# A hybrid diffusion step in fp32 on one core: the RG-LRU layer's units and engines reordered

## The chip, the cores and the metric

The kernel runs on one core of a Trainium2 chip. The metric is the device time of one execution in microseconds. The core's engines work through separate queues, each in order: TensorE (PE in the profile), VectorE (DVE), ScalarE (ACT), GpSimd (POOL), and SyncE (SP), which here only issues DMAs. They wait for one another through semaphores.

## The reference, cut to what matters

The reference is one inference step of a backbone of two layers over 128 context tokens and 512 latent tokens of width 1024. Layer 0 has an SSD mixer and a differential attention, layer 1 a bidirectional RG-LRU mixer; a gated ConvFFN follows each. The change concerns layer 1's mixer alone:

```python
def rglru_direction(xr, wa, ba, wx, bx, lam, h0, reverse):
    r = sigmoid(blockdiag(xr, wa) + ba)
    i = sigmoid(blockdiag(xr, wx) + bx)
    log_a = -RG_C * r * softplus(-lam)
    a = exp(log_a)
    u = sqrt(-expm1(2.0 * log_a)) * (i * xr)
    # linear scan h[n] = a[n] * h[n-1] + u[n], from h0, forward or backward
...
def odd_mixer(h, w_in, conv_w, conv_b, ...):
    gate, xr = split(h @ w_in, 2)
    xr = dwconv_centred(xr, conv_w, conv_b)
    yf = rglru_direction(xr, ..., False)
    yb = rglru_direction(xr, ..., True)
    return ((yf + yb) * gelu(gate)) @ w_out
```

The gate weights wa and wx are 16 blocks of 64x64 for each direction.

## The kernel before, in words

Activations lie transposed: 128 channels by NT = 644 columns (128 context tokens, a gap of 4 columns, 512 latent tokens). An fp32 product is made of three matmuls of a high and a low half (`mm3`, lines 469 to 473), each over two halves of 322 columns (`HALVES`). H is the list of eight pairs (`hhi[t]`, `hlo[t]`) of the mixer's input, and later of its output.

In `odd` (lines 1690 to 1882) 16 units make `h @ w_in`: x0 to x7 for the recurrence and g0 to g7 for the gate. The first three come from `gemm_parts` (line 642), the next twelve from `gemm` (line 484), the last from `last_gate` (line 1838). Their order is `lru_order` (line 426), and their weights are queued in the same order in `items`. A weight block of 128x1024 is loaded by SP (line 103), and `block` (line 122) splits it: ACT casts the high half (line 112) and POOL subtracts the low half in four pieces (line 117). Three blocks are split at a time, so the end of a unit releases the split of the unit three places on.

The program order is written out by a clock. `tick` (line 442) counts 2 for each of the 8 slices of K of a unit, so 16 for a unit, and fires what `after(n, f)` has queued for that tick (line 438); of two steps due at one tick, the one queued first goes first. The engines then take their instructions in that order, whatever the real time is.

Each x unit ends in `recur(t, ps)` (line 1730), which makes xr with one ACTIVATE and three VectorE steps (`conv_into`, line 519) and queues, for each direction d, at ticks from the table `LRU` (line 52; `LRU_LAST`, line 51, for t = 7):
- `product(d, i)` (line 1735): two matmuls of the gate weights `bd` with xr into the two small PSUM tiles, which ACT empties with tanh. The second gate (i = 1) is due 2 ticks behind the first. Behind the last product of a t, `gates_in(t + 3)` issues four DMAs for the gate weights of t + 3 on SP.
- `decay(d)` (line 1748): exp and tanh on ACT.
- `forms(d)` (line 1755): four steps on VectorE, the first of them inv * 0.5 + 0.5.
- `factors(d)` (line 1762): e = 2 inv - 1 on ACT, and a multiplication on POOL.

For both directions together follow `roots` (line 1767: square roots on ACT, which change its table, and multiplications on POOL), the scans (line 1775, VectorE; their sum on POOL) and `gated` (line 1788, VectorE). In the prediction (t, d, i) names a product and (t, d) the other steps. A g unit ends in `gelu(t, ps)` (line 1808): a square on ACT, a VectorE step, 5 ticks on a tanh on ACT, 7 ticks on a VectorE step.

From the last unit on, `give_h` (line 1831) hands the results over as H[t], one half of the columns at a time, with a cast on ACT and a subtraction on VectorE. Then `out_parts` (line 662) multiplies them with `w_out`: for its first three columns slices 0 to 5, then H[6], then H[7], which `ready` (line 1857) splits last.

Of the kernel before, what the change touches and what calls it, by code (L numbers as in the profile page):

```python
# [9 lines left out]
F32 = mybir.dt.float32  # L10
F32R = mybir.dt.float32r
AF = mybir.ActivationFunctionType
OP = mybir.AluOpType
# [34 lines left out]
FAST = (2, 2, 2, 2, 2, 1)  # L48
FFN = (4, 3, 4, 3, 4, 4)
LRU_RATES = 26  # L50
LRU_LAST = (10, 18, 4, 7, 12, 33, 41, 46)
LRU = (14, 31, 4, 7, 14, 51, 59, 66)
GIVE = (1, 4)
TAIL = (8, 5)
ATT = (6, 8, 4, 3, 3, 2, 3, 5, 7, 4)
# [7 lines left out]
def pieces(eng, op, out, a, b, n=PIECE):  # L63

    w = out.shape[-1]
    m = -(-w // n)
    for i in range(m):
        c = slice(w * i // m, w * (i + 1) // m)
        getattr(eng, op)(out[:, c], a[:, c], b[:, c])
# [13 lines left out]
class Weights:  # L83
# [38 lines left out]
    def block(self, i):  # L122
        raw = self.raw.pop(i)
        if self.items[i][3] == "held":
            hi, lo = (self.over.tile(list(raw.shape), F32R, name=f"{p}{i}") for p in ("hi", "lo"))
            self.nc.scalar.copy(hi, raw)
            for k0 in range(0, raw.shape[1], 2):
                q = slice(k0, min(raw.shape[1], k0 + 2))
                self.nc.gpsimd.tensor_sub(lo[:, q], raw[:, q], hi[:, q].bitcast(F32))
            self.parts[i] = hi, lo  # L130
        else:
            self.parts[i] = self.split(self.pool, raw, "w", self.n_part, self.nc.gpsimd)
        self.freed += 1

    def add_up(self, i):
# [105 lines left out]
def tile_hybrid_step(ctx: ExitStack, tc: tile.TileContext, a, o):  # L241
    nc = tc.nc
    k = Core()
# [72 lines left out]
    def fma(out, in0, scalar, in1, op0=OP.mult, op1=OP.add, **kw):  # L316
        nc.vector.scalar_tensor_tensor(out, in0, scalar, in1, op0=op0, op1=op1, **kw)  # L317
# [45 lines left out]
    def add_w(ap, r0, kt, c0, w=128, kind=None):  # L363
        items.append((ap[r0:r0 + 128 * kt, c0:c0 + w], kt, w, kind))
# [58 lines left out]

    ffn_starts = ffn_items(0)
    lw_in, lw_out = a["lru_w_in"][0], a["lru_w_out"][0]
    lru_order = [(what, t) for t in range(7) for what in "xg"]
    lru_order[13:] = [("x", 7), ("g", 6), ("g", 7)]
    for what, t in lru_order:
        add_w(lw_in, 0, 8, 128 * t + (1024 if what == "x" else 0))
    for n in range(8):  # L430
        add_w(lw_out, 0, 8, 128 * n, kind=held(n, N_STD[2]))
    ffn_items(1)
# [5 lines left out]
    def after(n, f):  # L438
        heapq.heappush(k.events, (k.clock + n, k.count, f))
        k.count += 1  # L440
# [73 lines left out]
    def conv(pool, ps, cw, cb, ntaps, t, nt, tag, bufs):  # L514
        out = pool.tile([128, NT], F32, name=tag, tag=tag, bufs=bufs)
        conv_into(out, ps, cw, cb, ntaps, t, nt)
        return out
# [32 lines left out]
    def mtile(tag=None):  # L550
        if tag is None:
            tag = k.m_tags.pop(0)
            k.m_tags.append(tag)
        return k.psum.tile([128, 512], F32, name="mt", tag=tag, bufs=1)
# [1135 lines left out]
    def odd():  # L1690
        with ExitStack() as st:
# [3 lines left out]
            pool = k.tmp = lctx.enter_context(tc.tile_pool(name="lru", bufs=1))  # L1695
# [3 lines left out]
            for b in bd:  # L1699
                nc.gpsimd.memset(b, 0.0)  # L1700
            cols = pool.tile([128, 6, 2, 8], F32, name="lcols")
            minus = pool.tile([128, 1], F32, name="minus")
            cb = [cols[:, i].rearrange("p d t -> p (d t)") for i in range(6)]
            hba, hbx, s2, s4 = range(4)

# [9 lines left out]
            def col(i, d, t):  # L1715
                return cols[:, i, d, t:t + 1]

            def gates_in(t):
                b = bd[t % 3]
                for i, nm in enumerate(("lru_wa", "lru_wx")):  # L1720
                    for s in range(2):
                        r = slice(64 * s, 64 * s + 64)
                        nc.sync.dma_start(b[r, :, i, r], a[nm][0, :, 2 * t + s].rearrange("d k j -> k d j"))

            def tmp(tag, bufs=1):
                return pool.tile([128, NT], F32, name=tag, tag=tag, bufs=bufs)

            gys, opened, k.scanned = {}, {}, set()

            def recur(t, ps):  # L1730

                xr = conv(pool, ps, "lru_cw", "lru_cb", 4, t, 8, "xr", 3)
                hs = []

                def product(d, i):
                    if i == 0:
                        hs.append([])
                    w = tmp("t%d" % i, 6)
                    hs[d].append(w)
                    for c0, c1 in HALVES:  # L1740
                        ps = mtile()
                        nc.tensor.matmul(ps[:, :c1 - c0], bd[t % 3][:, d, i], xr[:, c0:c1], start=True, stop=True)
                        nc.scalar.activation(w[:, c0:c1], ps[:, :c1 - c0], AF.Tanh, scale=0.5,
                                             bias=col(hba if i == 0 else hbx, d, t))
                    if d and i and t < 5:
                        gates_in(t + 3)

                def decay(d):
                    t1 = hs[d][0]
                    inv, e = tmp("inv", 3), tmp("e", 6)  # L1750
                    nc.scalar.activation(inv, t1, AF.Exp, scale=col(s4, d, t), bias=col(s4, d, t))
                    nc.scalar.activation(t1, t1, AF.Tanh, scale=col(s2, d, t), bias=col(s2, d, t))
                    hs[d] += [inv, e]

                def forms(d):
                    t1, t2, inv, e = hs[d]
                    nc.vector.tensor_scalar(inv, inv, 0.5, 0.5, op0=OP.mult, op1=OP.add)
                    fma(e, t1, 1.0, inv, op0=OP.subtract, op1=OP.mult)
                    fma(inv, e, 2.0, inv, op0=OP.add, op1=OP.mult)
                    fma(t2, t2, 1.0, xr, op0=OP.add, op1=OP.mult)  # L1760

                def factors(d):
                    t1, t2, inv, e = hs[d]
                    nc.scalar.activation(e, inv, AF.Identity, scale=2.0, bias=minus)
                    pieces(nc.gpsimd, "tensor_mul", t2, t2, inv)

                def roots():
                    for t1, t2, inv, e in hs:
                        nc.scalar.activation(t1, t1, AF.Sqrt, scale=-1.0)
                    for t1, t2, inv, e in hs:  # L1770
                        pieces(nc.gpsimd, "tensor_mul", t2, t2, t1)
                        nc.gpsimd.memset(e[:, NP:S0], 0.0)
                        nc.gpsimd.memset(t2[:, NP:S0], 0.0)

                def scan(d):
                    t1, t2, inv, e = hs[d]
                    if d == 0:
                        nc.vector.tensor_copy(t2[:, S0 - 1:S0], par("h0", t))
                        nc.vector.tensor_tensor_scan(t1, e, t2, 0.0, op0=OP.mult, op1=OP.add)
                        nc.vector.tensor_copy(last[:, 0, t:t + 1], t1[:, NP - 1:NP])  # L1780
                        return
                    nc.vector.tensor_tensor_scan(t1[:, ::-1], e[:, ::-1], t2[:, ::-1], par("h1", t),
                                                 op0=OP.mult, op1=OP.add)
                    nc.vector.tensor_copy(last[:, 1, t:t + 1], t1[:, 0:1])
                    y = gys[t] = tmp("gy", 8)
                    pieces(nc.gpsimd, "tensor_add", y, hs[0][0], t1)

                def gated():
                    if t not in opened:
                        after(1, gated)  # L1790
                        return
                    fma(gys[t], gys[t], 0.5, opened.pop(t), op0=OP.mult, op1=OP.mult)
                    k.scanned.add(t)

                pace = LRU_LAST if t == 7 else LRU
                for d in range(2):
                    at = pace[d]
                    after(at, lambda d=d: product(d, 0))
                    after(at + 2, lambda d=d: product(d, 1))
                    after(at + pace[2], lambda d=d: decay(d))  # L1800
                    after(at + pace[3], lambda d=d: forms(d))
                    after(at + pace[4], lambda d=d: factors(d))
                after(pace[5], roots)
                after(pace[6], lambda: scan(0))
                after(pace[6] + 1, lambda: scan(1))
                after(pace[7], gated)
# [11 lines left out]
                after(7, end)  # L1818

            for t in range(3):  # L1820
                gates_in(t)
            nc.gpsimd.memset(minus, -1.0)

            def sink(what, t):
                return lambda ps: (recur if what == "x" else gelu)(t, ps)
# [3 lines left out]
                sink(*u)(gemm(H)[0])  # L1829

            def give_h(t, c0, c1):
                if t not in k.scanned:
                    after(1, lambda: give_h(t, c0, c1))
                    return
                split_into(H[t], gys[t][:, c0:c1], c0, c1)
                k.n_given += 1
# [145 lines left out]
```

## Time and profile before

| | us |
|---|---|
| median of 3 runs | 2086.69 |
| lowest and highest run | 2076.94, 2088.32 |
| the profiled execution | 2080.74 |
| its span, first to last instruction | 2078.7 |
| RG-LRU layer, from the convolution of x1 to H[7] | 1336.0 to 1527.1 of the span |

In the profile's rows L471 is a line of the kernel. A row of the timeline gives start, duration, engine, line, operation, output<-input, and in brackets how long the engine had been idle and what released it. A row of the waits gives who waited for whom, how long in all, how often and the longest. A row of the groups gives busy time and the mean of one in ns, and behind a bar the idle time ahead of them.

### The profile page before, as it was taken

The page shows a single profiled execution, that of the slowest core. Times are in us where ns is not written, and L with a number is a line of the kernel's source. Part 1 is how long each engine was busy: PE and PEld are TensorE (multiplying, and loading weights), DVE is VectorE, ACT ScalarE, POOL GpSimd, SP SyncE. Part 2 cuts the span into 40 slices and gives each one's busy share as a digit, 9 for nine tenths or more (in the row PEclk, how much of TensorE's full clock was granted, in tenths as well). Part 3 has the DMA queues.
Part 4 walks back from the last instruction along what each step waited for, and adds up shares of the span by engine and source line. Part 5 has one row for each costly group of instructions (what it writes and reads, how often), then busy time and mean ns, then how long its engine had stood idle before and what let it go on. Part 6 is the DMA issues. An engine that isn't in the chain of part 4 may idle for free. (4 is left out here: it accounts for less than half of the span.)

```text
span 2078.7 us, 33613 instructions
## 1 busy us (share of the span) xinstructions
PE 1880.9 (90%) x12601; PEld 1719.6 (83%) x12601; DVE 1415.1 (68%) x2438; ACT 964.7 (46%) x1677; POOL 1184.0 (57%) x1528
## 2 busy tenths in 40 slices
PE   6878889999998999899999998988779899999997
PEld 4767668888887888798899997977679799999996
DVE  3477765655665337777778786676857778787874
ACT  3454453445444325433334344677725443443445
POOL 3235454333335445576557876478865577776772
PEclk9889999999999999999999999999889899999999
DMA  9554432112113342345542223112121122322221
GB/s 261 174 166 156 147 109 78 44 50 56 49 48 107 111 152 82 102 131 181 174 136 73 82 85 97 39 49 56 31 61 48 44 71 81 88 78 72 61 82 71
DMA packets 255577, 196.59 MB, mean 95 GB/s; under 512 B 13837, under 2 KB 233816, under 8 KB 255288
## 3 DMA queue, kind: packets, MB, share of 16 engines
q1 hardware_dynamic: 252664, 184.59, 29.6%
q0 software_dynamic: 2528, 7.13, 1.4%
q8 instruction: 99, 1.62, 0.3%
q10 hardware_dynamic: 224, 2.73, 0.3%
q14 instruction: 62, 0.51, 0.1%
HBM read 187.50 MB, written 6.92 MB: 94 GB/s over the span
## 5 line engine op out<-in xcount | busy, mean ns | idle before, releaser
L117 POOL TENSOR_TENSOR wlo<-wraw,whi 128x256 fp32r<-128x256 f32 (+1 forms) x835 | 710.7, 880 | 562.2 <-ACT whi L112 497.9
L471 PE MATMUL wide<-hhi,whi 128*128 128x322 f32 (+4 forms) x1072 | 358.7, 335 | 34.1 <-DVE X L317 15.2
L472 PE MATMUL wide<-hlo,whi 128*128 128x322 f32 (+4 forms) x1072 | 344.0, 321 | 7.5 <-DVE hlo L512 7.3
L473 PE MATMUL wide<-hhi,wlo 128*128 128x322 f32 (+4 forms) x1072 | 341.6, 319 | 0.0
L112 ACT CAST whi<-wraw 128x1024 fp32r<-128x1024 f32 (+1 forms) x259 | 217.4, 840 | 146.2 <-PE wide L473 71.1
L471 PEld LDWEIGHTS wide<-hhi,whi 128*128 128x128 f32 x1072 | 211.3, 197 | 52.9 <-ACT shi L112 15.4
L471 PE MATMUL gh<-hhi,whi 128*128 128x322 f32 (+3 forms) x688 | 232.1, 337 | 8.7 <-ACT zt L1178 8.7
L472 PEld LDWEIGHTS wide<-hlo,whi 128*128 128x128 f32 x1072 | 211.3, 197 | 12.2 <-DVE hlo L512 8.2
L472 PE MATMUL gh<-hlo,whi 128*128 128x322 f32 (+3 forms) x688 | 216.4, 315 | 1.3 <-DVE hlo L512 1.0
L473 PE MATMUL gh<-hhi,wlo 128*128 128x322 f32 (+3 forms) x688 | 215.9, 314 | 0.0
L473 PEld LDWEIGHTS wide<-hhi,wlo 128*128 128x128 f32 x1072 | 211.1, 197 | 0.0
L317 DVE SCALAR_TENSOR_TENSOR ft<-ft,PC 128x643 f32<-128x643 f32 x160 | 167.3, 1067 | 42.6 <-ACT ft L1550 40.6
L471 PE MATMUL wide<-hidh,whi 128*128 128x322 f32 (+2 forms) x600 | 191.3, 319 | 1.1 <-DVE ft L1608 1.1
L472 PE MATMUL wide<-hidl,whi 128*128 128x322 f32 (+2 forms) x600 | 187.0, 312 | 0.8 <-DVE hidl L512 0.8
L473 PE MATMUL wide<-hidh,wlo 128*128 128x322 f32 (+2 forms) x600 | 187.0, 312 | 0.0
L471 PEld LDWEIGHTS gh<-hhi,whi 128*128 128x128 f32 (+1 forms) x688 | 131.4, 191 | 33.7 <-issue 20.8
L317 DVE SCALAR_TENSOR_TENSOR X<-wide,modc,X 128x128 f32<-128x128 f32 (+3 forms) x276 | 128.0, 507 | 33.8 <-PE wide L473 33.8
L1550 ACT ACTIVATE ft<-ft,PC 128x644 f32<-128x644 f32 x80 | 73.9, 927 | 145.4 <-DVE ft L1615 135.3
L472 PEld LDWEIGHTS gh<-hlo,whi 128*128 128x128 f32 (+1 forms) x688 | 131.2, 191 | 2.4 <-DVE hlo L512 1.2
L473 PEld LDWEIGHTS gh<-hhi,wlo 128*128 128x128 f32 (+1 forms) x688 | 130.8, 190 | 0.6
L112 ACT CAST shi<-wsum 128x512 fp32r<-128x512 f32 x120 | 72.8, 617 | 123.8 <-DVE wsum L141 110.6
L471 PEld LDWEIGHTS wide<-hidh,whi 128*128 128x128 f32 x600 | 113.5, 189 | 14.5 <-issue 7.0
(379 smaller groups left out, 4606.6 us busy)
## 6 DMA issues: line engine op xcount, KB each, us to landing
wraw<-in_ffn_w_up_dram SPq DMA_DIRECT2D x88, 512.0 KB
mraw<-in_w_mod_dram SPq DMA_DIRECT2D x80, 512.0 KB
wraw<-in_ssd_attn_w_in_dram SPq DMA_DIRECT2D x42, 512.0 KB
wraw<-in_ffn_w_down_dram SPq DMA_DIRECT2D x96, 192.0 KB
E<-ad SPq DMA_DIRECT2D x16, 640.0 KB
mraw<-in_w_mod_dram SPq DMA_DIRECT2D x32, 256.0 KB
wraw<-in_ssd_attn_w_out_dram SPq DMA_DIRECT2D x16, 512.0 KB
wraw<-in_lru_w_in_dram SPq DMA_DIRECT2D x16, 512.0 KB
```

The costliest lines, as they stand in the source:

```text
L112: self.nc.scalar.copy(hi, src)
L117: low.tensor_sub(lo[:, q], src[:, q], hi[:, q].bitcast(F32))
L317: nc.vector.scalar_tensor_tensor(out, in0, scalar, in1, op0=op0, op1=op1, **kw)
L471: nc.tensor.matmul(ps[:whi.shape[-1], p0:p0 + c1 - c0], whi, xhi[:, c0:c1], start=start, stop=False)
L472: nc.tensor.matmul(ps[:whi.shape[-1], p0:p0 + c1 - c0], whi, xlo[:, c0:c1], start=False, stop=False)
L473: nc.tensor.matmul(ps[:whi.shape[-1], p0:p0 + c1 - c0], wlo, xhi[:, c0:c1], start=False, stop=stop)
L1550: after(at, lambda: nc.scalar.activation(out, u, AF.Identity, scale=par(cw, 2 * NF + t), bias=par(cb, t)))
```

## The change

It does the following.
- The order of the units becomes x0 g0 x1 x2 g1 x3 g2 x4 g3 x5 g4 x6 x7 g5 g6 g7.
- The low halves of the eight g weight blocks are subtracted by VectorE in one instruction.
- inv * 0.5 + 0.5 moves from VectorE (`forms`) to ACT (`decay`), with one more buffer for inv; e = 2 inv - 1 moves from ACT (`factors`) to VectorE (`forms`).
- The gate weights of t = 3 to 7 are loaded from ACT's queue, behind decay(1), instead of SP's, behind the last product.
- The second product is due 3 ticks behind the first, decay and forms one tick later than before, factors one tick later; x2 and x7 have tables of their own.
- H[6] is handed over only once `roots` of t = 7 has been issued.

```diff
-LRU_LAST = (10, 18, 4, 7, 12, 33, 41, 46)
-LRU = (14, 31, 4, 7, 14, 51, 59, 66)
+LRU_LAST = (20, 33, 5, 8, 13, 44, 52, 58)
+LRU_NEXT = (23, 39, 5, 8, 15, 59, 67, 74)
+LRU = (14, 31, 5, 8, 15, 51, 59, 66)
...
-            self.parts[i] = self.split(self.pool, raw, "w", self.n_part, self.nc.gpsimd)
+            low = self.nc.vector if self.items[i][3] == "vector" else self.nc.gpsimd
+            self.parts[i] = self.split(self.pool, raw, "w", self.n_part, low)
...
-    lru_order = [(what, t) for t in range(7) for what in "xg"]
-    lru_order[13:] = [("x", 7), ("g", 6), ("g", 7)]
+    lru_order = [(w[0], int(w[1])) for w in "x0 g0 x1 x2 g1 x3 g2 x4 g3 x5 g4 x6 x7 g5 g6 g7".split()]
     for what, t in lru_order:
-        add_w(lw_in, 0, 8, 128 * t + (1024 if what == "x" else 0))
+        add_w(lw_in, 0, 8, 128 * t + (1024 if what == "x" else 0), kind="vector" if what == "g" else None)
...
-            def gates_in(t):
+            def gates_in(t, eng):
...
-                        nc.sync.dma_start(b[r, :, i, r], a[nm][0, :, 2 * t + s].rearrange("d k j -> k d j"))
+                        eng.dma_start(b[r, :, i, r], a[nm][0, :, 2 * t + s].rearrange("d k j -> k d j"))
...
-                    if d and i and t < 5:
-                        gates_in(t + 3)
...
                 def decay(d):
                     t1 = hs[d][0]
-                    inv, e = tmp("inv", 3), tmp("e", 6)
+                    inv, e = tmp("inv", 4), tmp("e", 6)
                     nc.scalar.activation(inv, t1, AF.Exp, scale=col(s4, d, t), bias=col(s4, d, t))
+                    nc.scalar.activation(inv, inv, AF.Identity, scale=0.5, bias=half)
                     nc.scalar.activation(t1, t1, AF.Tanh, scale=col(s2, d, t), bias=col(s2, d, t))
                     hs[d] += [inv, e]
+                    if d and t < 5:
+                        gates_in(t + 3, nc.scalar)
 
                 def forms(d):
                     t1, t2, inv, e = hs[d]
-                    nc.vector.tensor_scalar(inv, inv, 0.5, 0.5, op0=OP.mult, op1=OP.add)
                     fma(e, t1, 1.0, inv, op0=OP.subtract, op1=OP.mult)
                     fma(inv, e, 2.0, inv, op0=OP.add, op1=OP.mult)
                     fma(t2, t2, 1.0, xr, op0=OP.add, op1=OP.mult)
+                    nc.vector.tensor_scalar(e, inv, 2.0, -1.0, op0=OP.mult, op1=OP.add)
 
                 def factors(d):
                     t1, t2, inv, e = hs[d]
-                    nc.scalar.activation(e, inv, AF.Identity, scale=2.0, bias=minus)
                     pieces(nc.gpsimd, "tensor_mul", t2, t2, inv)
...
                         nc.scalar.activation(t1, t1, AF.Sqrt, scale=-1.0)
+                    k.rooted = t
...
-                pace = LRU_LAST if t == 7 else LRU
+                pace = LRU_LAST if t == 7 else LRU_NEXT if t == 2 else LRU
...
-                    after(at + 2, lambda d=d: product(d, 1))
+                    after(at + 3, lambda d=d: product(d, 1))
...
-                gates_in(t)
-            nc.gpsimd.memset(minus, -1.0)
+                gates_in(t, nc.sync)
+            nc.gpsimd.memset(half, 0.5)
...
-                if t not in k.scanned:
+                if t not in k.scanned or (t == 6 and k.rooted < 7):
```

## Rows read from the trace of the kernel before

**Rows 1.** The page, busy time, share of the span and instructions of each engine.
```profile
PE 1880.9 (90%) x12601; PEld 1719.6 (83%) x12601; DVE 1415.1 (68%) x2438; ACT 964.7 (46%) x1677; POOL 1184.0 (57%) x1528
```
**Rows 2.** Stretches xr4-xr5, tail: length, PE, PEld, DVE, ACT, POOL; PE clock, DMA, GB/s.
```profile
1409.40:1433.90 24.50, 21.13 (x112) 19.23 (x111) 17.22 (x20) 16.72 (x25) 19.61 (x28) 0.86 0.17 48
...
1494.20:1527.10 32.90, 12.73 (x56) 11.86 (x54) 28.78 (x34) 13.60 (x25) 30.32 (x40) 0.71 0.11 32
```
**Rows 3.** Timeline of TensorE, 1418 to 1432 and 1455 to 1495 us.
```profile
1420.24 2.51 PE L1742 MATMUL mt<-xr,bd 128*128 128x322 f32 x4 [3.37 <-ACT t L1743]
...
1422.81 0.47 PE L472 MATMUL wide<-hlo,whi 128*128 128x322 f32 x1
...
1426.15 0.31 PE L473 MATMUL wide<-hhi,wlo 128*128 128x322 f32 x1
...
1431.05 0.31 PE L473 MATMUL wide<-hhi,wlo 128*128 128x322 f32 x1
...
1462.42 1.25 PE L1742 MATMUL mt<-xr,bd 128*128 128x322 f32 x4
...
1463.65 0.31 PE L472 MATMUL wide<-hlo,whi 128*128 128x322 f32 x1
```
**Rows 4.** Waits of TensorE, 1300 to 1540 us: total, times, longest.
```profile
PE mt L1742 <- ACT t L1743: 18.7, 10, 3.4
PE wide L471 <- ACT hhi L508: 12.9, 1, 12.9
PE wide L472 <- DVE hlo L512: 7.3, 1, 7.3
```
**Rows 5.** Waits of all engines, 1300 to 1540 us.
```profile
ACT e L1764 <- DVE inv L317: 38.5, 8, 9.6
...
DVE gl L317 <- ACT gl L1810: 18.4, 6, 5.5
POOL wlo L117 <- ACT whi L112: 16.7, 8, 4.2
```
**Rows 6.** Groups of instructions by line, 1308 to 1545 us.
```profile
L317 DVE SCALAR_TENSOR_TENSOR t<-t,xr 128x644 f32<-128x644 f32 x16 | 18.0, 1124 | 0.0
L317 DVE SCALAR_TENSOR_TENSOR inv<-e,inv 128x644 f32<-128x644 f32 x16 | 17.9, 1116 | 0.6
L317 DVE SCALAR_TENSOR_TENSOR e<-t,inv 128x644 f32<-128x644 f32 x16 | 16.9, 1055 | 2.5 <-ACT t L1752 1.2
...
L1751 ACT ACTIVATE inv<-t,lcols 128x644 f32<-128x644 f32 x16 | 14.8, 927 | 0.0
...
L1779 DVE TENSOR_TENSOR_SCAN t<-e,t 128x644 f32<-128x644 f32 x8 | 13.1, 1638 | 0.3
...
L1757 DVE TENSOR_SCALAR inv<-inv 128x644 f32<-128x644 f32 x16 | 12.6, 790 | 3.9 <-ACT inv L1751 3.9
L512 DVE TENSOR_TENSOR hlo<-gy,hhi 128x388 fp32r<-128x388 f32 (+2 forms) x15 | 12.0, 851 | 0.5 <-ACT hhi L508 0.5
```
**Rows 7.** Line 119, a low half on VectorE elsewhere in the kernel: minimum/median/maximum in ns.
```profile
L119 DVE TENSOR_TENSOR slo<-wsum,shi x80: 673/998/1262, 832.5 to 2013.4; 128x512 fp32r<-128x512 f32 x80
```
**Rows 8.** A DMA issued from ACT's queue elsewhere in the kernel.
```profile
L1881 ACTq DMA_DIRECT2D out_new_lru_fwd_dram<-lt x1: 556/556/556, 1579.5 to 1579.5; - x1
```
**Rows 9.** Timeline of VectorE: the convolutions of x1, x3 and x6.
```profile
1336.99 2.73 DVE L317 SCALAR_TENSOR_TENSOR xr<-wide,PC,xr 128x642 f32<-128x642 f32 x3 [4.54 <-ACT xr L521]
...
1388.65 2.73 DVE L317 SCALAR_TENSOR_TENSOR xr<-wide,PC,xr 128x642 f32<-128x642 f32 x3
...
1459.45 2.73 DVE L317 SCALAR_TENSOR_TENSOR xr<-wide,PC,xr 128x642 f32<-128x642 f32 x3
```
**Rows 10.** Timeline of ACT: the roots of t = 0.
```profile
1361.10 1.28 ACT L1769 ACT_TABLE_LOAD   x1
1362.40 1.38 ACT L1769 ACTIVATE t<-t 128x644 f32<-128x644 f32 x2
```
**Rows 11.** Tile inv: a step of forms, minimum/median/maximum in ns.
```profile
L317 DVE SCALAR_TENSOR_TENSOR inv<-e,inv x16: 828/1194/1249, 1341.8 to 1499.0; 128x644 f32<-128x644 f32 x16
```

More of the change, by code (lines that the diff above doesn't have):

```diff
@@ L1701, in odd @@
             cols = pool.tile([128, 6, 2, 8], F32, name="lcols")
-            minus = pool.tile([128, 1], F32, name="minus")
+            half = pool.tile([128, 1], F32, name="half")
             cb = [cols[:, i].rearrange("p d t -> p (d t)") for i in range(6)]
@@ L1722, in gates_in @@
                         r = slice(64 * s, 64 * s + 64)
-                        nc.sync.dma_start(b[r, :, i, r], a[nm][0, :, 2 * t + s].rearrange("d k j -> k d j"))
+                        eng.dma_start(b[r, :, i, r], a[nm][0, :, 2 * t + s].rearrange("d k j -> k d j"))
             def tmp(tag, bufs=1):
                 return pool.tile([128, NT], F32, name=tag, tag=tag, bufs=bufs)
-            gys, opened, k.scanned = {}, {}, set()
+            gys, opened, k.scanned, k.rooted = {}, {}, set(), -1
             def recur(t, ps):
```

## The prediction

> **What bounds the kernel now.** First the page: TensorE is busy for nine tenths of the span [rows 1], so a change in the RG-LRU layer can win only the time in which TensorE waits there or runs at 1.2 instead of 2.4 GHz ("half clock" below). Then the layer, cut by the convolutions of x1 to x7 [rows 2]: the middle stretch shown takes 24.5 us (three more are like it) for two units of 7.1 us (48 matmuls at (1431.05 - 1426.15) / 33 gaps = 0.148 us each [rows 3]) and four gate products of 1.1 us (1462.42 to 1463.65 is 1.23 with the slower matmul behind it, less 0.15 [rows 3]). That is 18.6 us of work. The last stretch, 32.9 us, holds 12.7 us of matmuls. Who ends TensorE's waits [rows 4]: ten times a tanh of ACT (18.7 us); in the tail H[0]'s low half (7.3) and H[6]/H[7] (12.9). Behind the tanh stands another wait [rows 5]: eight times ACT stood, 38.5 us in all, before the last step of `factors`, which needs VectorE, with the next tanh queued behind it. In the tail VectorE is busy 28.8 of 32.9 us [rows 2]: there its list of work sets the end.
>
> **The order after the change.** A unit is 16 ticks, so the code gives the tick of every step. Before, x7 comes out at tick 224 and the products end at 256; after, at 208 and 256: one unit more lies behind x7 and can cover its recurrence. t = 0 and 1 keep their ticks, t = 2 moves forward by 6, and from t = 3 on all is 16 ticks earlier. Two orders turn as well. `decay(t+1, 0)` fell one tick ahead of `roots(t)`; with 5 in place of 4 both fall on the same tick, and the roots, queued first, go first. And scan(6) and the roots of 7 now stand among the hand-overs of H[0] to H[5]. The condition on `rooted` changes no order: roots(7) is at tick 252, and H[6] waits for gated(6) at 258 anyway.
>
> **Cost, edit by edit.** The halving (0.5, 0.5) goes to ACT and the decay (2, -1) to VectorE: each engine swaps one 128x644 step for another (0.79 us on VectorE [rows 6]). What goes is ACT's wait for VectorE; next late is VectorE itself.
> Eight low halves go from POOL (4 pieces each) to VectorE, 128x1024 at once. The nearest row is the 128x512 subtraction of 0.673 to 1.262 us [rows 7]; doubled, less some 0.14 for the start, 1.2 to 2.4 us. I take 1.3, near the lower end, since POOL does less meanwhile. Each stands in VectorE's queue ahead of an x convolution or a gelu.
> Twenty gate-weight DMAs leave SP for ACT's queue, where an issue of this kernel took up to 0.56 us [rows 8]. SP's relief is worth nothing: TensorE waited for no weight DMA here. On ACT four issues stand behind each `decay(t, 1)`, ahead of the next tanh: 0 to 2.2 us. I take 0.7 once, at t = 0, where ACT has no slack; later VectorE is later than ACT. Their wait for the last product that read the buffer is over, since that product's tanh stands ahead of them.
> The Trainium skill ("Trainium Kernel Development and Optimization", Key Constraints) says that issuing DMAs from several engines saves only the sequencer's issue time. That speaks against a gain; no run here shows it yet, and my zero agrees.
>
> **Front, to xr3.** x1 ends at about 1334.3, two tanhs and the conv of ACT ahead of VectorE's part of xr1 at 1336.99 [rows 9]; the tanhs now stand behind the conv. From there ACT sets the pace. Up to the end of decay(1, 1) it has conv xr1 and xr2 (1.7), three casts (2.85), seven tanh pairs at 0.95 (6.65), four decays at 2.65 (10.6: exp and tanh 0.93 each [rows 6], halving 0.8), one square (0.6), the roots of 0 (4.0: load 1.28, square roots 1.37 [rows 10], load 1.28) and the DMAs 0.7: 27.1 us, and 4.7 of waiting for products: 31.8. Then VectorE: forms 4.1 (0.79 + 1.055 + 1.116 + 1.124 [rows 6]), gelu 0.75, two scans with their copies 3.6 (2 x 1.64 [rows 6] and 0.3), forms 4.1, low half 1.3, conv 2.65: 16.5. xr3 stands at 1334.3 + 48.3 = 1382.6, against 1388.65 + 2.7 = 1391.3 before [rows 9]: **-8.7**.
>
> **Middle, xr3 to xr6.** One cycle runs from P(t,0,0), released by xr, to the next xr: product, 12 matmuls, product and both tanhs 4.8; roots 4.0; exp, halving, tanh 2.65; forms 4.1; gelu 0.75; scans 3.6; low half 1.3; conv 2.65: 23.9. The first of three cycles has its scans behind xr4 (-3.6), the second no low half (-1.3): 66.8. TensorE, done sooner with its 18.6 us, then waits 4 to 5 us for xr in two of them and comes back at half clock: after the wait of 3.37 us a product with the matmul behind it took 2.57 instead of 1.23 (1420.24 to 1422.81 [rows 3]). I add 1.2 twice: 69.2 against 70.8 before (1391.3 to 1459.45 + 2.65 = 1462.1 [rows 9]): **-1.6**. So ACT's 38.5 us of waits go, and the time is spent on roots that stand ahead of forms.
> The load in the row is followed by the square root after 0.02 us [rows 10]. The Trainium skill ("ScalarE: Activation LUTs", What ACT_TABLE_LOAD costs) adds a drain of 1.38 us to each load; by that the roots would cost 6.7 us and three cycles 8 us more, and the trace disagrees.
>
> **Tail, xr6 to H[7].** VectorE's list: gated(4) 1.1, forms(5,1) 4.1, low half 1.3, xr7 2.65, four forms 16.4, three pairs of scans 10.8, three gelus 4.5, three gated 3.4, fourteen hand-overs 12 (0.851 each [rows 6]): 56.3. Waits: 2.5 for decay(6,0) behind the roots of 5, 1.4 and 1.8 for the last tanhs, 0.4 for POOL, and H[7]'s cast 0.5: 62.9 against 65.0 (1462.1 to 1527.1): **-2.1**. The third gate unit and its products fit beneath (41 us of TensorE). H[6] is no longer last, so its 9 matmuls of 0.18 are done ahead: **-1.6**.
>
> **Sum.** 8.7 + 1.6 + 2.1 + 1.6 = 14.0 us. The profiled execution took 2080.74 (span 2078.7): 2066.7. The median of the runs shown is 5.95 higher, which would give 2072.7; I take about the middle, 2069 us. About 0.5% (10 us) is what a measurement of this kernel can tell from no change.
>
> **Rivals.**
> *Nothing measurable: half clock eats it.* ACT's wait is only renamed, into TensorE's for xr. If each is followed by half clock through both products and the 12 matmuls (2.5 us), in four cycles and not two halves, 7.6 us go again, 2 more in the front, and with low halves at 2.4 us (four on the path, 4.4) all of it: 2083. For it: the clock of 0.86 in the stretch with the wait of 3.37 us [rows 2]. Against: TensorE has 5 us of slack in a cycle.
> *Slower: VectorE takes over POOL's wait for the cast.* POOL waited 16.7 us in 8 waits for ACT's cast of the weights, 4.2 at most [rows 5]. VectorE's low half now stands in that wait, with forms and scans queued behind. At 2.1 us each for eight the gain is gone; at 4.2 each 33.6 us come on top: 2103; from 3 us each (2094) it decides. Against: VectorE waits at this place already (for gl 18.4 us [rows 5]), so the cast is mostly covered.
> *Much faster: POOL's relief speeds VectorE.* The same forms step takes 0.828 us at least and 1.249 at most [rows 11], the latter while POOL runs. If half of that excess goes along the path (front 1, middle 3, tail 4, hand-overs and scans 5), 13 us more: 2056. Against: in the tail POOL keeps its work. The Trainium skill ("SBUF — State Buffer", SBUF: two separate sides) calls the port pair that VectorE and GpSimd share an exclusive lock; by that one hold of about 1.3 us takes the place of four of POOL's, and the row agrees that one slows the other.
>
> **Chances.** Forecast 0.45, much faster 0.20, nothing measurable 0.22, slower 0.13. The forecast's own range is 2058 to 2078 (the low half's two prices, the issues', the clock's); about nine tenths of it is faster by over 0.5%. Faster 0.60; same 0.05 + 0.22 = 0.27; slower 0.13. The range leaves out the worst of the slower rival and the best of the faster: 2048 to 2088.
>
> **What would show it.** Right: no wait of ACT for inv; TensorE's longest waits in the middle end with xr, 4 to 5 us each; xr3 some 9 us earlier, xr3 to xr6 about as long as before; H[7] 63 us behind xr6, with VectorE busy nine tenths of that. Wrong: cycles of 20 us (then the order on ACT matters less than I say); waits of VectorE for the cast of over 3 us ahead of its low halves (the slower rival); gaps on ACT of 2 us or more behind decay(t,1) (the DMAs cost more than I took).

## The result, and the profile after

Seven runs of the changed kernel have a median of 2071.95 us (2066.80 to 2074.41), seven of the kernel before beside them 2085.34 (2076.94 to 2088.32): a ratio of 0.9946, 95% interval 0.9928 to 0.9965, so 7 to 15 us less. The forecast was 2069, with 14.0 us as the sum of its terms and "faster" as the likeliest. The medians differ by 13.4 us, close to that sum; the layer itself, measured below in one execution of each kernel, by 10.0 us. The interval holds both, so how close 13.4 lies to 14.0 is partly luck.

In the changed kernel the lines stand one or two further down (the products at L1743, their tanhs at L1744, `fma` at L319, the roots at L1770). First the page's busy row [rows 1], then one cycle of the middle (xr4 to xr5) and the last stretch up to H[7] [rows 2]; the columns are those of before.

```profile
PE 1885.9 (91%) x12601; PEld 1721.9 (83%) x12601; DVE 1421.0 (69%) x2446; ACT 967.5 (47%) x1679; POOL 1157.9 (56%) x1496
```
```profile
1406.20:1432.00 25.80, 21.92 (x133) 20.09 (x131) 21.13 (x26) 17.06 (x24) 24.12 (x32) 0.99 0.15 41
1492.90:1522.70 29.80, 18.23 (x63) 15.59 (x63) 26.47 (x33) 11.67 (x22) 26.38 (x36) 0.66 0.12 35
```

The cycle is no shorter than before (25.8 against 24.5 us). The waits of 1300 to 1540 us tell what took the place of [rows 4, 5]:

```profile
ACT t L1744 <- PE mt L1743: 25.8, 13, 6.7
DVE e L319 <- ACT t L1752: 24.4, 7, 6.3
...
PE mt L1743 <- ACT t L1744: 10.0, 5, 5.1
...
PE mt L1743 <- issue: 7.6, 2, 4.0
...
DVE wlo L120 <- ACT whi L113: 5.2, 2, 3.8
...
PE wide L472 <- ACT hhi L509: 2.4, 2, 2.1
```

ACT's 38.5 us of waiting for inv are gone. Now VectorE waits for ACT (24.4, most of it forms for a decay that stands behind roots), and ACT for TensorE (25.8). TensorE's waits for a tanh fell from 18.7 to 10.0 us, and no wait for H[6] is left (the 2.4 us are two other high halves').

The program ahead of the layer is unchanged, yet the first convolution (x0's on ACT) began at 1325.03 us before and 1327.52 after; over the 14 kernels profiled here this start lies anywhere from 1319.75 to 1327.52. So I measure **the stage**: from there to the first addition into X behind H[7]. It took 207.3 us before and 197.3 after. The timeline of VectorE has its marks [rows 9], first the last two of before:

```profile
1526.69 1.88 DVE L512 TENSOR_TENSOR hlo<-gy,hhi 128x256 fp32r<-128x256 f32 x3 [0.47 <-ACT hhi L508]
1532.33 1.00 DVE L317 SCALAR_TENSOR_TENSOR X<-wide,modc,X 128x128 f32<-128x128 f32 x3 [3.76 <-PE wide L473]
```
```profile
1382.43 2.72 DVE L319 SCALAR_TENSOR_TENSOR xr<-wide,PC,xr 128x642 f32<-128x642 f32 x3
...
1403.59 2.72 DVE L319 SCALAR_TENSOR_TENSOR xr<-wide,PC,xr 128x642 f32<-128x642 f32 x3
...
1420.47 0.83 DVE L319 SCALAR_TENSOR_TENSOR e<-t,inv 128x644 f32<-128x644 f32 x1 [3.04 <-ACT t L1752]
...
1429.33 2.73 DVE L319 SCALAR_TENSOR_TENSOR xr<-wide,PC,xr 128x642 f32<-128x642 f32 x3
...
1444.97 0.83 DVE L319 SCALAR_TENSOR_TENSOR e<-t,inv 128x644 f32<-128x644 f32 x1 [4.88 <-ACT t L1752]
...
1453.53 2.72 DVE L319 SCALAR_TENSOR_TENSOR xr<-wide,PC,xr 128x642 f32<-128x642 f32 x3
...
1461.34 1.39 DVE L120 TENSOR_TENSOR wlo<-wraw,whi 128x1024 fp32r<-128x1024 f32 x1 [1.40 <-ACT whi L113]
...
1470.56 0.83 DVE L319 SCALAR_TENSOR_TENSOR e<-t,inv 128x644 f32<-128x644 f32 x1 [5.19 <-ACT t L1752]
...
1521.07 0.83 DVE L319 SCALAR_TENSOR_TENSOR gy<-gy,gl 128x644 f32<-128x644 f32 x1 [1.15 <-POOL gy L70]
1522.69 0.83 DVE L513 TENSOR_TENSOR hlo<-gy,hhi 128x644 fp32r<-128x644 f32 x1 [0.80 <-ACT hhi L509]
1524.78 1.39 DVE L319 SCALAR_TENSOR_TENSOR X<-wide,modc,X 128x128 f32<-128x128 f32 x4 [1.25 <-PE wide L474]
```

H[7] is marked by the start of its low half, 1522.69 after. Before, the row at 1526.69 holds three low halves: the two parts of H[6], the second of them from 1527.10, and H[7]'s from 1527.74. The 1527.1 that the prediction takes for H[7] is thus H[6]'s second part, and its 65.0 us for the tail before are 65.6.

| part of the stage | before | after | change | forecast |
|---|---|---|---|---|
| x0's convolution to xr3 (its last step's end) | 66.3 | 57.6 | -8.7 | -8.7 |
| xr3 to xr6 | 70.8 | 71.1 | +0.3 | -1.6 |
| xr6 to H[7] (1527.7 before, 1522.7 after) | 65.6 | 66.4 | +0.9 | -2.1 |
| H[7] to the addition into X | 4.6 | 2.1 | -2.5 | -1.6 |
| sum | 207.3 | 197.3 | -10.0 | -14.0 |

Behind it nothing changed (+0.2). The profiled execution itself, 2074.41, lies only 6.3 us below that of before: its layer began 2.5 us later, the latest of all fourteen.

TensorE's clock shows in its timeline behind the waits. In the first rows it had worked; in the next ones it had waited 3.65 us for xr6 (shown as "issue": the wait ends with xr):

```profile
1409.13 1.25 PE L1743 MATMUL mt<-xr,bd 128*128 128x322 f32 x4
...
1456.35 2.48 PE L1743 MATMUL mt<-xr,bd 128*128 128x322 f32 x4 [3.65 <-issue]
...
1459.17 0.47 PE L474 MATMUL wide<-hhi,wlo 128*128 128x322 f32 x1
1459.44 0.47 PE L472 MATMUL wide<-hhi,whi 128*128 128x322 f32 x1
...
1461.85 0.68 PE L1743 MATMUL mt<-xr,bd 128*128 128x322 f32 x1
```

The stretch up to the next product, and one behind it (columns as in [rows 2]):

```profile
1456.35:1461.85 5.50, 5.50 (x16) 4.70 (x17) 4.06 (x6) 2.65 (x4) 2.12 (x4) 0.50 0.07 21
1462.90:1468.00 5.10, 5.10 (x35) 5.00 (x34) 2.39 (x3) 5.03 (x7) 1.88 (x5) 1.00 0.37 103
```

The product took 2.48 instead of 1.25 us, and the matmuls behind it came every 0.27 us instead of 0.15 [rows 3], up to the next product. The granted clock was 0.50 there, the level of 1.2 GHz, and 1.00 behind it. Waits of 5.13, 2.99 and 3.96 us (1370.56, 1401.01, 1432.16) were each followed by a product of 2.5 us too.

### The profile page after: what moved, and what is told of

Read it like the earlier page. It is cut to its first block, busy times and chain, and to the rows that moved or that the text cites. A ratio compares the mean times of both kernels' runs of the same rounds, so it can differ in the third digit from the quotient of the medians.

```text
span 2071.4 us, 33556 instructions
## 1 busy us (share of the span) xinstructions
PE 1885.9 (91%) x12601; PEld 1721.9 (83%) x12601; DVE 1421.0 (69%) x2446; ACT 967.5 (47%) x1679; POOL 1157.9 (56%) x1496
## 5 line engine op out<-in xcount | busy, mean ns | idle before, releaser
L118 POOL TENSOR_TENSOR wlo<-wraw,whi 128x256 fp32r<-128x256 f32 (+1 forms) x803 | 678.3, 874 | 560.1 <-ACT whi L113 496.3
L319 DVE SCALAR_TENSOR_TENSOR ft<-ft,PC 128x643 f32<-128x643 f32 x160 | 167.2, 1066 | 42.7 <-ACT ft L1551 40.8
L472 PEld LDWEIGHTS gh<-hhi,whi 128*128 128x128 f32 (+1 forms) x688 | 131.8, 192 | 34.1 <-issue 21.2
L319 DVE SCALAR_TENSOR_TENSOR X<-wide,modc,X 128x128 f32<-128x128 f32 (+3 forms) x276 | 128.1, 507 | 30.2 <-PE wide L474 30.2
## 6 DMA issues: line engine op xcount, KB each, us to landing
wraw<-in_ffn_w_down_dram SPq DMA_DIRECT2D x96, 192.0 KB
```

Source lines behind the costliest of these rows:

```text
L118: low.tensor_sub(lo[:, q], src[:, q], hi[:, q].bitcast(F32))
L472: nc.tensor.matmul(ps[:whi.shape[-1], p0:p0 + c1 - c0], whi, xhi[:, c0:c1], start=start, stop=False)
```

## The experiments

Each starts from the changed kernel unless said otherwise. The stage of each is from its one profile; the ratio is to runs of the kernel before made beside it. Two limits go with the table. The intervals of the ratios are 5 to 11 us wide: those of e4, e6, e7, e9, e11 and e12 hold the changed kernel's 0.9946, so none of these can be told from it by itself; but all six kernels with later roots lie below it. And equal instructions don't take equal times: up to xr7 e8 runs the program of the changed kernel, and its marks lay up to 0.7 us earlier; the clock adds about 1 us more (e4). So differences of the stage of about 1 us, those among e9 to e12 above all, show nothing by their size.

| run | stage, us | ratio to before, 95% interval |
|---|---|---|
| before; changed | 207.3; 197.3 | 1; 0.9946 [0.9928, 0.9965] |
| e1 old order | 207.4 | 0.9991 [0.9978, 1.0003] |
| e2 old swap | 204.0 | 0.9984 [0.9973, 0.9995] |
| e3 low halves on POOL | 199.7 | 0.9962 [0.9948, 0.9976] |
| e4 gate DMAs on SP | 196.2 | 0.9935 [0.9909, 0.9960] |
| e5 order alone | 205.2 | 0.9980 [0.9964, 0.9996] |
| e6 roots 2 ticks later | 192.0 | 0.9941 [0.9920, 0.9962] |
| e7 roots 3 ticks later | 193.2 | 0.9937 [0.9916, 0.9957] |
| e8 whole hand-overs | 201.5 | 0.9978 [0.9964, 0.9991] |
| e9 = e6 and e4 | 191.8 | 0.9929 [0.9913, 0.9946] |
| e10 = e9, tail reordered | 191.7 | 0.9917 [0.9901, 0.9933] |
| e11 = e9, three low halves on POOL | 192.2 | 0.9928 [0.9909, 0.9946] |
| e12 = e10, a w_out low half on VectorE | 191.6 | 0.9928 [0.9905, 0.9951] |

**e1: the order of before, with all the rest.**

```diff
-LRU_LAST = (20, 33, 5, 8, 13, 44, 52, 58)
+LRU_LAST = (10, 18, 5, 8, 13, 33, 41, 46)
...
-    lru_order = [(w[0], int(w[1])) for w in "x0 g0 x1 x2 g1 x3 g2 x4 g3 x5 g4 x6 x7 g5 g6 g7".split()]
+    lru_order = [(what, t) for t in range(7) for what in "xg"]
+    lru_order[13:] = [("x", 7), ("g", 6), ("g", 7)]
...
-                pace = LRU_LAST if t == 7 else LRU_NEXT if t == 2 else LRU
+                pace = LRU_LAST if t == 7 else LRU
...
-                if t not in k.scanned or (t == 6 and k.rooted < 7):
+                if t not in k.scanned:
```

> The stage is measured from the convolution of x0 on ACT to the first addition into X behind the hand-over of H[7]: 207.3 us before, 197.3 after the change. Here the units stand in their old order, with the old table for t = 7 and the old hand-over rule; all else is as after the change. My theory says that the gain is the order's: xr3 came 8.7 us earlier since the x units of t = 3 to 7 stand one place further forward. Then the stage goes back to 206 to 210 us. The rival: the gain is that of the swap of halving and decay, which took ACT's 38.5 us of waits away; then the stage stays at 197 to 201 us, whatever the order.

The stage took 207.4 us, as before: without the order, and with the roots where the change puts them, nothing is left of the gain. The old order with later roots (as in e6) wasn't tried. Two of its waits say why: VectorE stands before decays that ACT has queued behind roots, and TensorE at the end before H[6], as before the change:

```profile
DVE e L319 <- ACT t L1753: 32.6, 8, 7.6
...
PE wide L473 <- ACT hhi L510: 13.3, 1, 13.3
```

**e2: the halving on VectorE, the decay on ACT, as before.** For t = 7 the gap's factors are then written behind the step that clears them, so there the backward scan carries over the gap (in e5 too).

```diff
-                    nc.scalar.activation(inv, inv, AF.Identity, scale=0.5, bias=half)
...
+                    nc.vector.tensor_scalar(inv, inv, 0.5, 0.5, op0=OP.mult, op1=OP.add)
...
-                    nc.vector.tensor_scalar(e, inv, 2.0, -1.0, op0=OP.mult, op1=OP.add)
...
+                    nc.scalar.activation(e, inv, AF.Identity, scale=2.0, bias=half)
...
-            nc.gpsimd.memset(half, 0.5)
+            nc.gpsimd.memset(half, -1.0)
```

> Halving goes back to VectorE and the last step of factors to ACT; order, low halves and gate DMAs stay as after the change. My theory: ACT again waits for forms(t, 1) ahead of the tanh of P(t+1, 0, 0), some 4 us behind xr in each cycle, less the halving's 0.8 us on ACT; over three cycles and the tail the stage grows by 8 to 16 us, to 205 to 213. The rival: roots ahead of decay hold the cycle anyway, so the swap is worth nothing: 196 to 199 us, with ACT's waits for inv back at 20 us or more and no later end.

The stage grew by 6.7 us, somewhat under the theory's range and far from the rival. ACT's wait is back, with TensorE's waits for tanhs behind it:

```profile
ACT e L1765 <- DVE inv L319: 28.5, 10, 7.7
PE mt L1743 <- ACT t L1744: 23.5, 11, 5.5
```

**e5: the order alone** (tables and the condition on H[6] kept; the swap of e2, the low halves of e3 and the DMAs of e4 as before).

> The new order of the units with its tables and the hand-over rule, and nothing else of the change: halving on VectorE, the last step of factors on ACT, low halves on POOL, gate DMAs on SP. (For t = 7 the factors of the gap's four columns are then written after they are zeroed, so its backward scan carries over the gap; that changes no duration.) The order alone was worth 10.1 us where the swap stood beside it, and the swap 6.7 where the order did. My theory: both belong together, since the new order lets ACT's waits for forms fall into each cycle; alone it gives 2 to 5 us: the stage is 202 to 206 us long (207.3 before, 197.3 after). The rival: the parts simply add; then order alone stays at 197 to 200.

205.2: the order alone gives 2.1 of the 10.0 us, all the rest without it nothing (e1). The gain belongs to the parts together: the order puts a unit behind x7, and without the swap (e2) ACT again waits 28.5 us for VectorE. Order and swap without the other edits weren't run.

**e3: the low halves back on POOL.**

```diff
-        add_w(lw_in, 0, 8, 128 * t + (1024 if what == "x" else 0), kind="vector" if what == "g" else None)
+        add_w(lw_in, 0, 8, 128 * t + (1024 if what == "x" else 0), kind=None)
```

> The eight low halves of the g weights go back to POOL; all else is as after the change. My theory: four of them, 1.2 to 1.7 us each, lie on VectorE's chain (ahead of xr3, xr4, xr6, xr7), and POOL has room for eight times 3 to 4 us but in the tail: the stage gets 2 to 6 us shorter, 191 to 195. The rival: POOL has no room, its multiplications by the roots come later and the scans wait for them (now at most 0.6 us each); then the stage is 4 us or more longer, 201 or above, and waits of VectorE for POOL at the scans grow past 1 us each.

The theory was wrong: 199.7, so the low halves on VectorE are worth 2.4 us. xr3 did come 1.9 us earlier, but xr5 3.1 later. POOL's pieces of a weight block stood ahead of the sum gy, and VectorE's gated step, queued ahead of forms, waited for that; first POOL's timeline, then VectorE's:

```profile
1409.87 4.25 POOL L118 TENSOR_TENSOR wlo<-wraw,whi 128x256 fp32r<-128x256 f32 x4
1414.07 1.86 POOL L70 TENSOR_TENSOR gy<-t,t 128x214 f32<-128x214 f32 x3
```
```profile
1415.97 1.26 DVE L319 SCALAR_TENSOR_TENSOR gy<-gy,gl 128x644 f32<-128x644 f32 x1 [3.15 <-POOL gy L70]
```

**e4: the gate weights' DMAs back on SP,** at the same place of the program.

```diff
-                        gates_in(t + 3, nc.scalar)
+                        gates_in(t + 3, nc.sync)
```

> The gate weights of t = 3 to 7 are loaded from SP's queue again, at the new place; all else is as after the change. My theory: the issues cost ACT only what shows as gaps behind decay(t, 1) where ACT leads, 1.2 + 1.0 us at t = 0 and 1; the stage gets 1 to 3 us shorter, 194 to 196. The rival: SP's relief was worth something, since weight loads queue behind these DMAs; then the stage is 2 us or more longer, 199 or above.

196.2, so the sign fits, but not the place. From x0's convolution, xr3 came at the same time as in the changed kernel (54.9 us to its start in both), and ACT's gap behind the first four issues is there without them: in the changed kernel and in e4 the same tanh began 30.79 us behind x0's convolution, after the same gap.

```profile
1358.31 1.07 ACT L1744 ACTIVATE t<-mt,lcols 128x322 f32<-128x322 f32 x2 [1.24 <-DMA bd<-in_lru_wa_dram]
```
```profile
1352.42 1.07 ACT L1744 ACTIVATE t<-mt,lcols 128x322 f32<-128x322 f32 x2 [1.25 <-PE mt L1743]
```

The 1.0 us come behind xr6, where no gate DMA is left: TensorE waited the same 3.64 us, but was back at 0.15 us a matmul from the seventh on (granted clock 0.54 up to 1454.3, then 1.00), where it stayed at 0.27 in the changed kernel, and VectorE's wait for decay(6,0) was 4.00 instead of 5.19 us.

```profile
1450.63 2.28 PE L1743 MATMUL mt<-xr,bd 128*128 128x322 f32 x4 [3.64 <-issue]
...
1454.30 0.31 PE L472 MATMUL wide<-hhi,whi 128*128 128x322 f32 x1
1454.44 0.31 PE L473 MATMUL wide<-hlo,whi 128*128 128x322 f32 x1
```

Behind the next four issues ACT was 1.1 us later than in e4, but the decay that VectorE waited for stands ahead of them, and its forms began 40.9 us behind x0's convolution in both. So in this order the issues on ACT, 0.60 to 0.72 us each, cost nothing on the path up to xr3, and the 1.0 us can't be put down to them. The Trainium skill ("Trainium Kernel Development and Optimization", Key Constraints) says that issuing DMAs from several engines saves issue time alone. e4 agrees: with SP as the issuer xr3 came no later (54.9 us).

**e6 and e7: the roots behind decay(t+1, 0), and later still.** With the roots at 51, ACT changes its table and takes two square roots while VectorE waits for a decay behind them.

```diff
-LRU = (14, 31, 5, 8, 15, 51, 59, 66)
+LRU = (14, 31, 5, 8, 15, 53, 59, 66)
```

> One number differs from the change: the roots of t = 0, 1, 3 to 6 are due at 53 ticks in place of 51, so decay(t+1, 0) goes ahead of them again. My theory: the roots' 4.0 us leave the chain from xr to xr; the scans behind still need them, so 2 to 3 us of each cycle are won, in two to three cycles and once in the tail: 188 to 193 us for the stage. The rival: VectorE's own work, some 20 us in a cycle of 24, holds the cycle, and the scans wait for POOL instead: 195 to 198 us, with waits of VectorE for POOL at the scans of 2 us or more.

> As the run before, with 54 ticks: the roots go behind the tanh of the gelu too, so that VectorE's last gelu step doesn't wait for them. My theory: another 0 to 2 us, 187 to 192 us. The rival: the scans come as late as the roots, and the stage is 1 to 3 us longer than with 53.

The largest gain in the stage: 192.0, that is 5.3 us more than the change gave, 3.5 of them between xr3 and xr6. It rests on one profile of each kernel: the ratios of whole runs, 0.9941 and 0.9946, can't be told apart. Of VectorE's 24.4 us of waiting for decays 8.5 are left:

```profile
DVE e L319 <- ACT t L1752: 8.5, 5, 2.1
```

One tick more (54, behind the gelu's tanh too) was 1.2 us longer, hardly more than equal programs differ by, but its waits grew: the forward scans waited 5.3 instead of 3.0 us for POOL's part of the roots, and forms 12.5 instead of 8.5 us for decays.

**e8: H[0] to H[5] handed over whole,** to shorten VectorE's list.

```diff
-                    for t in range(7):
-                        after(1 + t, lambda t=t, c=(c0, c1): give_h(t, *c))
...
+                for t in range(7):
+                    after(1 + t, lambda t=t: give_h(t, 0, NT))
```

> After the change, but H[0] to H[6] are each handed over once, 644 columns wide, instead of in two parts of 388 and 256; the first slices of w_out wait for H[0] to H[5] as before. My theory of the tail: VectorE's list of work sets its end. Fourteen subtractions of 0.85 us become seven of 0.85 to 1.3, so 3 to 6 us go: 191 to 194 us for the stage, though TensorE gets H[0] 4 to 6 us later. The rival: the late H[0] sets the end, since TensorE has 63 matmuls of 0.18 us to make behind it at half clock; then 197 us or above.

The theory was wrong: 201.5. H[7] did come earlier, but by 0.6 us only (194.6 behind x0's convolution, 195.2 in the changed kernel), and TensorE, which got each H[t] later, waited five times, ran at half clock (0.53 granted on average from 1493 to 1520) and became the end itself. Four of the five waits, and VectorE's wait for that end:

```profile
1500.43 0.69 PE L473 MATMUL wide<-hlo,whi 128*128 128x388 f32 x1 [6.67 <-DVE hlo L513]
1503.41 0.69 PE L473 MATMUL wide<-hlo,whi 128*128 128x388 f32 x1 [1.63 <-DVE hlo L513]
1507.57 0.69 PE L473 MATMUL wide<-hlo,whi 128*128 128x388 f32 x1 [1.63 <-DVE hlo L513]
1513.30 0.69 PE L473 MATMUL wide<-hlo,whi 128*128 128x388 f32 x1 [4.39 <-DVE hlo L513]
...
1526.04 2.04 DVE L319 SCALAR_TENSOR_TENSOR X<-wide,modc,X 128x128 f32<-128x128 f32 x6 [6.05 <-PE wide L474]
```

**e9: the edits of e6 and e4 together.**

> The changed kernel with the roots two ticks later (LRU 51 to 53) and the gate weights back on SP. Theory: the two gains lie at different places, the roots' in the middle cycles and at the tail's start, the DMAs' on ACT ahead of the first tanhs of t = 0 to 2, so they add: from the convolution of x0 on ACT to the first addition into X 190 to 192 us (197.3 changed, 192.0 and 196.2 with each alone), and a time of 2063 to 2067 us. Rival: behind later roots ACT has slack, so that the DMAs cost nothing there any more: 192 to 193.5.

191.8: by its number within the theory's range, but only 0.2 us below e6; the gains don't add. At the front the issues do cost something here, since the roots stand right behind them: xr3 came 1.4 us earlier than in e6 (53.1 against 54.5). Two cycles later that was gone (xr6 at 123.2, in e6 122.1): TensorE waited 5.56 us for xr5 instead of 3.34.

**e10: the tail of e9 reordered,** so that ACT issues decay(7,1) and the tanh of g6 ahead of the roots of 6.

```diff
-LRU_LAST = (20, 33, 5, 8, 13, 44, 52, 58)
+LRU_LAST = (20, 31, 5, 8, 13, 44, 52, 58)
...
-                pace = LRU_LAST if t == 7 else LRU_NEXT if t == 2 else LRU
+                pace = LRU_LAST if t == 7 else LRU_NEXT if t == 2 else LRU[:5] + (54,) + LRU[6:] if t == 6 else LRU
```

> The kernel of the run before it, and besides, for the tail alone, the second direction's products of t = 7 two ticks earlier and the roots of t = 6 one tick later, so that ACT issues decay(7,1) and the gelu's tanh of g6 ahead of the roots of 6. Theory: VectorE's list sets the tail, and its two waits there for ACT (3.1 us for the gelu's tanh, 1.7 for decay(7,1), seen with the roots at 53) go: 2 to 4.5 us from the stage, 186 to 190. Rival: the list's end hangs on POOL (its low half of the w_out weights ahead of gy of t = 7), so that VectorE only waits later: within 1 us of the run before it.

The rival was right: 191.7. Both waits for ACT went, and VectorE waited for POOL instead, first for the multiplication behind the later roots, in the end for gy, which POOL has behind the low half of a w_out block (4.34 us at 1501.40):

```profile
1485.30 0.15 DVE L1780 COPY t<-PC 128x1 f32<-128x1 f32 x1 [2.41 <-POOL t L1775]
...
1507.77 0.83 DVE L319 SCALAR_TENSOR_TENSOR gy<-gy,gl 128x644 f32<-128x644 f32 x1 [1.14 <-POOL gy L70]
```

Its median, 2064.54 us, is the lowest of all; it can't be told from e9's 2065.85 by these runs.

**e11: e9 with the low halves of g0, g1 and g2 on POOL.**

```diff
-        add_w(lw_in, 0, 8, 128 * t + (1024 if what == "x" else 0), kind="vector" if what == "g" else None)
+        add_w(lw_in, 0, 8, 128 * t + (1024 if what == "x" else 0), kind="vector" if what == "g" and t > 2 else None)
```

> The kernel with the later roots and the gate weights on SP, with the low halves of g0, g1 and g2 back on POOL and those of g3 to g7 on VectorE. Theory: with all eight on POOL the front to xr3 became 1.9 us shorter and the middle 3.1 us longer, so the first three are better on POOL: 1 to 2 us from the stage of the run with both edits. Rival: POOL's four pieces stand ahead of the multiplications of t = 0 and 1 there and the gain goes into the scans' waits: within 0.7 us, or longer.

192.2, the rival: xr3 came at 53.1 us in e9 and here, so the 1.9 us that e3 won at the front are no longer there once the roots are later.

**e12: e10 with that low half of w_out on VectorE.**

```diff
-        add_w(lw_out, 0, 8, 128 * n, kind=held(n, N_STD[2]))
+        add_w(lw_out, 0, 8, 128 * n, kind="vector" if n == 2 else held(n, N_STD[2]))
```

> The kernel of e10, with the low half of the third w_out block subtracted by VectorE in one step, which POOL did in four pieces (4.3 us) ahead of the sum gy of t = 7. Theory: POOL's list has become one of two ends of the tail. It holds VectorE's last gated step back by 1.1 us, and TensorE waits 3.3 us for this low half and then runs at half clock up to H[7]; both go, for 1.2 to 1.7 us more in VectorE's list, much of which lies in its two waits for POOL (2.4 and 0.6 us): from the convolution of x0 on ACT to the first addition into X 189 to 191 us (191.7 before). Rival: VectorE's list alone is the end and pays the whole step: 192 to 193.5.

191.6, between the two, and by its size no different from e10. VectorE paid 1.66 us for the step and still finished H[7] 0.9 us earlier than in e10 (188.7 against 189.6), so POOL did hold it back. But TensorE, no longer stopped halfway by the low half, was done early, waited 4.96 us for H[7] and came back at half clock (0.50 granted from 1511.8 to 1516.0, 1.00 behind H[7] in e10): a matmul of 0.69 us, where it was 0.44 in e10.

```profile
1511.82 0.69 PE L472 MATMUL wide<-hhi,whi 128*128 128x388 f32 x1 [4.96 <-ACT hhi L509]
```

## Why the prediction was right, and where its terms were not

**Front: right to the tenth, in part by luck.** ACT sets the pace there and its list was counted instruction by instruction. Two errors inside went against each other: the issues on ACT, taken at 0.7 us, cost nothing on the path (e4), and the low half ahead of xr3 took 1.67 us (at 1380.84) instead of 1.3.

**Middle: the step that failed is the cycle's first one,** "from P(t,0,0), released by xr". In the first and third cycle that holds. They took 21.2 and 24.2 us where 20.3 and 23.9 stood, without the half clock. The second, forecast at 22.6, took 25.8: xr4 was there at 1406.3, but the product began at 1409.13. TensorE had waited 2.99 us for a tanh, had come back at half clock, and still had matmuls of its unit ahead of the product:

```profile
1401.01 2.51 PE L1743 MATMUL mt<-xr,bd 128*128 128x322 f32 x4 [2.99 <-ACT t L1744]
```
```profile
1401.00:1404.70 3.70, 3.69 (x11) 2.89 (x12) 3.53 (x5) 3.66 (x6) 3.70 (x5) 0.55 0.50 142
```

These 2.8 us were in no term. Of the two additions of 1.2 us for half clock one came: in the third cycle, behind the wait of 3.96 us, forms began 12.8 us after the product (1432.16 to 1444.97), in the second, at full clock, 11.3. That the third cycle still took 24.2 us is luck: forms took 2.8 us in it, with POOL idle, and not 4.1.

**What bounds the middle was named, but not followed.** The prediction said that ACT's 38.5 us would be spent on "roots that stand ahead of forms". It took this as given. e6 shows that it was a choice of two ticks in a table, worth 5.3 us of the stage.

**Tail: the waits were mis-sized.** VectorE's waits behind xr6 sum to 12.2 us (1.40 + 5.19 + 0.81 + 1.67 + 0.61 + 0.53 + 1.15 + 0.80) where 6.6 stood; its list, 66.4 - 12.2 = 54.2, was 2.1 below the 56.3. So it was busy for 82% of the tail, not for nine tenths. The largest miss is decay(6,0) behind the roots of 5: 5.19 instead of 2.5, as TensorE's product and the 12 matmuls behind it ran at half clock. Not foreseen at all was 1.40 for the cast ahead of the low half. For POOL it waited 2.3 (0.61 + 0.53 + 1.15) where 0.4 stood; POOL has a w_out block ahead of gy:

```profile
1514.71 4.33 POOL L118 TENSOR_TENSOR wlo<-wraw,whi 128x256 fp32r<-128x256 f32 x4
1519.00 2.04 POOL L70 TENSOR_TENSOR gy<-t,t 128x214 f32<-128x214 f32 x3
```

**H[6] no longer last: right, and larger.** -2.5 instead of -1.6: its matmuls are done ahead, and TensorE had waited 12.89 us before H[6] and 0.37 before H[7] now, so that what is left is faster too (0.44 us for H[7]'s first matmul, 0.69 for H[6]'s before).

**The rivals.** "Half clock eats it" was half right: four waits, each followed by a product of 2.5 us, and the middle's gain gone; the front kept its own. "VectorE takes over POOL's wait" was not: it waited 5.2 us in two waits for the cast, and e3 shows the move to be a gain. One of the two, 3.81 us ahead of xr2, is over the 3 us that the prediction gave as this rival's sign; it cost little, since with the low halves on POOL (e3) xr2 came only 0.35 us earlier. "POOL's relief speeds VectorE" was not either. The first step of forms is slower than before, the second faster [rows 6], and the low half, at 1.22 us at least, has a mean of 1.47. POOL was still at work beside most of them: the second step took 0.83 us where POOL did little or nothing meanwhile (four of sixteen before, six after) and 1.15 to 1.25 us elsewhere. The groups of 1310 to 1545 us:

```profile
L319 DVE SCALAR_TENSOR_TENSOR e<-t,inv 128x644 f32<-128x644 f32 x16 | 17.7, 1106 | 24.4 <-ACT t L1752 24.4
L319 DVE SCALAR_TENSOR_TENSOR inv<-e,inv 128x644 f32<-128x644 f32 x16 | 16.8, 1049 | 0.6
...
L120 DVE TENSOR_TENSOR wlo<-wraw,whi 128x1024 fp32r<-128x1024 f32 x7 | 10.3, 1465 | 5.5 <-ACT whi L113 5.2
```

That the condition on `rooted` changes nothing rests on the order of the ticks; it wasn't tried by itself.

## What to carry to other kernels

When a wait between two in-order engines is removed, look at what stands behind it in the queue of the engine that was freed: here the next thing on ACT was a table change with two square roots, and in the stage moving it by two ticks gave half as much again as the whole change. Edits that reorder and edits that free an engine have to be priced together (the order alone 2.1 us, the rest without it 0, together 10.0). And measure the stage beside the run: the start of the layer, behind the same instructions, varied by 7.8 us between executions, almost as much as was to be measured. One profile of a stage has a spread too, here up to about 1 us.

## What was not expected of the hardware

A gain on VectorE can be lost through TensorE's clock. In e12 TensorE had less to wait for on the way, so it waited longer at the end, and matmuls at a granted clock of 0.50 instead of 1.00 (0.69 instead of 0.44 us for the first) took back the 0.9 us that H[7] had won. The same wait need not be followed by the same clock: after 3.65 and 3.64 us before the same product, the matmuls stayed at 0.27 us for the whole of the twelve in one execution and were back at 0.15 from the seventh in the other. What decided between the two stays open.
